# Low parts of the fill tiles' weights, made by a second, adding transfer in place of a subtraction on VectorE

## The chip, the cores and the metric

The kernel runs on one core of one Trainium2 chip. The metric is the device time of one execution in microseconds (us); lower is better. Engines are named as in the profile: PE (TensorE, matrix multiplication), PEld (its weight loads), DVE (VectorE), ACT (ScalarE), POOL (GpSimd), and SP (SyncE), which here only issues transfers (DMAs).

## The reference, cut to what matters

A trunk of two layers over 512 tokens with 1024 channels, in fp32. In each layer the normalized input goes through one wide projection `w_in`; its columns feed four mixers (RWKV7, gated linear attention, a linear recurrence, HGRN2); their outputs are joined, projected by `w_out`, normalized and added; a gated feed-forward block follows.

```python
for l in range(DEPTH):
    h = _rms_norm(x, norm_mix_pre[l])
    proj = h @ w_in[l]
    p_a, p_b, p_c, p_d = _split(proj, (RWKV_COLS, GLA_COLS, LRU_COLS, HGRN_COLS))
...
    mixed = jnp.concatenate([y_a, y_b, y_c, y_d], axis=-1).astype(x.dtype) @ w_out[l]
    x = x + _rms_norm(mixed, norm_mix_post[l])
    h = _rms_norm(x, norm_ffn_pre[l])
    gate, up = jnp.split(h @ ffn_w_gate_up[l], 2, axis=-1)
    x = x + _rms_norm((jax.nn.silu(gate) * up) @ ffn_w_down[l], norm_ffn_post[l])
```

## The kernel before, in words

**Products in three parts.** Every large product is computed as three products of parts. A weight tile of 128 output columns by 1024 inputs is loaded as `ws` (512 KB, L387, a transfer issued by SP). ACT rounds it to the high part `wh` (L388), and DVE subtracts, `wl = ws - wh`, the low part (L389). The activations are split likewise into `hh` and `hl`. For each of the eight 128-row blocks k, `mm3` (L398) issues wh·hh, wl·hh, wh·hl: 24 matmuls for a tile, and already the second one reads `wl`. All this is one helper, `load_w`, used for every weight.

**Fill tiles.** In each layer the work between the input normalization and `w_out` is called the merge here: 62 to 291 us of the span in layer 0 and 756 to 991 us in layer 1. There the generator `fill()` makes the column tiles of `w_in` still missing (20 for each layer go through its call of `gemm`), while four generators make the mixers: `rwkv`, `hgrn`, `gla`, `lru`. `merge` takes steps from these five by a string of digits, one string for each layer (`ORDER`; 0 is the fill, 1 to 4 the mixers). That sets the order in which the program is written. A scheduler, which simulates the engines while the program is built, then sets the order of the instructions on each engine from it. Once set, each engine runs its instructions strictly in that order, so one that waits holds up those behind it. The same holds for the transfers that POOL issues: they stand in POOL's own row of instructions.

**Memory.** Tiles live in 47 blocks, given out and reused; a tile name such as `block_wl` in the profile says what stands in a block at that time.

**Lines named further down.** L608 to L610 compute the RWKV decay (DVE, then ACT with loads of its function tables); L656 the first product of its blocks (`A`), L952 a product on POOL that L955 (`dk`) reads on PE; L734 a masking on POOL that L742 (`ap`) reads; L759 and L808 (DVE) rearrange blocks for L829 (`pq` on PE); L707 (`dot`) is a small product on PE; L1060, L1179 and L442/L443 are ACT functions at the mixers' ends; L1250 takes a finished fill tile out of PE's accumulators.

## Time and profile before

| | us |
|---|---|
| median of three runs | 1411.95 |
| lowest and highest | 1409.92 to 1412.04 |
| the profiled execution's own time | 1410.65 |
| its span in the trace | 1408.9 |
| busy in the span: PE | 1359.2 (96%) |
| busy: DVE | 792.9 (56%) |
| busy: ACT | 633.5 (45%) |
| busy: POOL | 81.0 (6%) |

The span runs from the first to the last recorded instruction. A busy share is an average over stages of different kinds: in the feed-forward stages PE is nearly always busy; in the two merges it has to share the time with long chains of small instructions on DVE, ACT and POOL. "PEclk" in a table by stretches is the granted clock of PE as a share of the full one (1.00 is 2.4 GHz, 0.50 is 1.2 GHz).

### The profile page before, as it was taken

How to read it: one execution, taken by the hardware profiler on the slowest of the kernel's cores; microseconds unless marked ns; L12 is line 12 of the kernel's file. 1: busy time of each engine (PE TensorE's matmuls, PEld its weight loads, DVE VectorE, ACT ScalarE, POOL GpSimd, SP SyncE). 2: the span in 40 equal slices, each digit the busy share in tenths (PEclk: the TensorE clock that was granted, in tenths of full speed). 3: DMA queues.
4: the chain of work that ended last, by engine and by line, in shares of the span. 5: the costliest groups of instructions: out<-in, count | busy, mean ns of one | idle time of the engine just before them, and what ended most of it. 6: DMA issues, size and time to landing. Idle time of an engine off the chain costs nothing.

```text
span 1408.9 us, 20225 instructions
## 1 busy us (share of the span) xinstructions
PE 1359.2 (96%) x8284; PEld 1150.8 (82%) x8284; DVE 792.9 (56%) x1241; ACT 633.5 (45%) x1035; POOL 81.0 (6%) x71
## 2 busy tenths in 40 slices
PE   7999998999999999999999999989999999999996
PEld 7877877779988888888897778776998888888886
DVE  7598848746834344412666996586286444433234
ACT  6546458555623232322556374676464232223232
POOL 0130102000000000000002300120000000000000
PEclk9989999999999999999999899999999999999999
DMA  7101202314422222433542111133053313233342
GB/s 269 59 30 30 75 16 90 92 46 135 165 90 90 75 90 75 145 91 94 173 149 60 45 45 61 40 96 107 24 171 116 124 45 114 70 101 121 106 130 85
DMA packets 51692, 131.75 MB, mean 94 GB/s; under 512 B 4752, under 2 KB 23776, under 8 KB 51600
## 3 DMA queue, kind: packets, MB, share of 16 engines
q1 hardware_dynamic: 50400, 128.47, 28.5%
q8 instruction: 65, 1.06, 0.3%
q10 hardware_dynamic: 960, 0.95, 0.2%
q0 software_dynamic: 240, 1.05, 0.2%
q14 instruction: 27, 0.22, 0.0%
HBM read 122.06 MB, written 8.39 MB: 93 GB/s over the span
## 4 chain that ended last, share of the span: by engine, by line
PE 79%; DVE 9%; ACT 8%; DMA 2%; issue 2%; POOL 0%; SPq 0%; DVEq 0%; ACTq 0%; POOLq 0%
PE g L398 69%; PE lv L999 2%; DMA block_ws<-in_w_in_dram 1%; DVE block_wl L389 1%; PE nrm L451 1%; ACT block_wh L388 1%; DVE block_att L1005 1%; DMA block_x<-in_xT_dram 1%; PE A L656 1%; PE px L836 1%; ACT block_ws L994 0%; PE ap L742 0%; DVE block_ws L1018 0%; PE pq L829 0%; ACT L1179 0%
## 5 line engine op out<-in xcount | busy, mean ns | idle before, releaser
L398 PE MATMUL g<-block_h,block_wh 128*128 128x512 f32 (+1 forms) x1738 | 496.7, 364 | 9.0 <-ACT block_h L479 7.6
L398 PEld LDWEIGHTS g<-block_h,block_wh 128*128 128x128 f32 x1738 | 317.1, 192 | 61.6 <-ACT block_h L479 8.1
L398 PE MATMUL g<-block_h,block_wl 128*128 128x512 f32 (+1 forms) x1126 | 340.8, 360 | 0.7 <-DVE block_wl L389 0.6
L398 PE MATMUL g<-block_wl,block_wh 128*128 128x512 f32 (+1 forms) x827 | 255.7, 353 | 0.2 <-ACT block_wh L388 0.2
L398 PEld LDWEIGHTS g<-block_h,block_wl 128*128 128x128 f32 x1126 | 210.3, 192 | 32.6 <-DVE block_wl L389 1.9
L388 ACT CAST block_wh<-block_ws 128x1024 fp32r<-128x1024 f32 (+1 forms) x124 | 128.4, 1038 | 226.2 <-DMA block_ws<-in_w_dn_dram 66.2
L398 PE MATMUL g<-block_wl,block_wl 128*128 128x512 f32 (+1 forms) x607 | 184.9, 351 | 0.0
L398 PEld LDWEIGHTS g<-block_wl,block_wh 128*128 128x128 f32 x827 | 151.4, 191 | 22.8 <-ACT block_wh L388 1.0
L389 DVE TENSOR_TENSOR block_wl<-block_ws,block_wh 128x1024 fp32r<-128x1024 f32 (+1 forms) x82 | 102.9, 1257 | 83.6 <-ACT block_wh L388 68.2
L398 PEld LDWEIGHTS g<-block_wl,block_wl 128*128 128x128 f32 x607 | 111.1, 190 | 15.4 <-issue 0.7
L388 ACT CAST block_wl<-block_ws 128x1024 fp32r<-128x1024 f32 (+1 forms) x46 | 47.4, 1031 | 93.6 <-PE g L398 35.4
L398 PE MATMUL g<-block_g,block_wl 128*128 128x512 f32 (+1 forms) x314 | 82.5, 344 | 0.0
L398 PE MATMUL g<-block_g,block_wh 128*128 128x512 f32 (+1 forms) x280 | 81.2, 347 | 0.0
L389 DVE TENSOR_TENSOR block_wl<-block_ws,block_wl 128x1024 fp32r<-128x1024 f32 (+1 forms) x32 | 38.1, 1191 | 50.1 <-ACT block_wl L388 45.8
L398 PEld LDWEIGHTS g<-block_g,block_wl 128*128 128x128 f32 x314 | 53.6, 189 | 7.2 <-issue 0.2
L398 PEld LDWEIGHTS g<-block_g,block_wh 128*128 128x128 f32 x280 | 48.6, 189 | 6.6 <-issue 0.2
L389 DVE TENSOR_TENSOR block_wh<-block_ws,block_wh 128x1024 fp32r<-128x1024 f32 (+1 forms) x29 | 34.6, 1192 | 32.8 <-ACT block_wh L388 27.2
L398 PE MATMUL g<-block_wh,block_wh 128*128 128x512 f32 (+1 forms) x145 | 46.6, 342 | 0.0
L398 PE MATMUL g<-block_wh,block_wl 128*128 128x256 f32 (+1 forms) x133 | 37.9, 337 | 0.4 <-DVE block_wl L389 0.4
L580 POOL TENSOR_SCALAR block_sq<-block_sq 64x512 f32<-64x512 f32 x2 | 1.2, 618 | 579.1 <-DVE block_cum L1250 521.2
L398 PE MATMUL g<-block_h,block_y 128*128 128x512 f32 x90 | 33.7, 389 | 0.0
L398 PE MATMUL g<-block_g,block_h 128*128 128x512 f32 (+1 forms) x100 | 33.0, 366 | 0.0
(1096 smaller groups left out, 2122.1 us busy)
## 6 DMA issues: line engine op xcount, KB each, us to landing
block_ws<-in_w_gu_dram SPq DMA_DIRECT2D x78, 512.0 KB, 3.6
block_ws<-in_w_in_dram SPq DMA_DIRECT2D x48, 512.0 KB, 3.7
block_ws<-in_w_dn_dram SPq DMA_DIRECT2D x39, 512.0 KB, 3.6
block_ws<-in_w_dn_dram SPq DMA_DIRECT2D x18, 384.0 KB, 3.1
xs<-block_x SPq DMA_DIRECT2D x18, 256.0 KB, 3.9
block_x<-xs SPq DMA_DIRECT2D x18, 256.0 KB, 4.0
block_x<-in_xT_dram SPq DMA_DIRECT2D x14, 256.0 KB, 5.3
block_ws<-in_w_out_dram SPq DMA_DIRECT2D x6, 512.0 KB, 3.7
```

The lines of the kernel that those rows point to most:

```text
L388: nc.scalar.copy(out=wh, in_=ws)
L389: nc.vector.tensor_sub(out=wl, in0=ws, in1=wh.bitcast(F32))
L398: nc.tensor.matmul(ps, lhsT=w[:, i, :], rhs=h[i], start=(first and n == 0), stop=(last and n == len(steps) - 1))
L451: nc.tensor.matmul(ps, lhsT=self.ones, rhs=acc[:, s], start=(s == 0), stop=(s == 1))
L580: nc.gpsimd.tensor_scalar(out=low[64:128, :], in0=low[64:128, :], scalar1=0.5, scalar2=0.5, op0=ALU.mult, op1=ALU.add)
L656: nc.tensor.matmul(ps[:, j * P:(j + 1) * P], lhsT=bk[ct][p0:p0 + 64, c_ * P:(c_ + 1) * P], rhs=ar[ct][p0:p0 + 64, c_ * P:(c_ + 1) * P], st ...
L836: nc.tensor.matmul(ps[:, g * P:g * P + P], lhsT=n21[h][:, g * P:(g + 1) * P], rhs=pq[h][:, g * P:g * P + P], start=True, stop=True)
L999: nc.tensor.matmul(ps[:, j * nh * 64:(j + 1) * nh * 64], lhsT=Kt[ct][:, g * P:(g + 1) * P], rhs=qr[:, g].rearrange("p h c -> p (h c)"), st ...
L1005: nc.vector.copy_predicated(out=av[:, :, :, 1, :], mask=m, data=pv)
```

## The change

For the fill tiles alone, `load_w` no longer subtracts on DVE. ACT writes the negative of the high part, `wl = -wh`, and then POOL issues a second transfer of the same 512 KB of `w_in` from HBM, which adds what it brings to what stands in `wl`: again ws - wh. All other weights keep the subtraction. The two strings of `ORDER` are altered too.

```diff
-    def load_w(self, src, nk):
+    def load_w(self, src, nk, adding=False):
...
             nc.sync.dma_start(out=ws, in_=src)
             nc.scalar.copy(out=wh, in_=ws)
-            nc.vector.tensor_sub(out=wl, in0=ws, in1=wh.bitcast(F32))
+            if adding:
+                nc.scalar.activation(out=wl, in_=wh.bitcast(F32), func=AF.Copy, scale=-1.0)
+                nc.gpsimd.dma_start(out=wl, in_=src, accum_op=ALU.add)
+            else:
+                nc.vector.tensor_sub(out=wl, in0=ws, in1=wh.bitcast(F32))
...
-    def gemm(self, src, hs, nk=KD, c=slice(0, T), later=0, keep=None):
+    def gemm(self, src, hs, nk=KD, c=slice(0, T), later=0, keep=None, adding=False):
...
-                w = self.load_w(src[:, k0:k0 + n, :], n)
+                w = self.load_w(src[:, k0:k0 + n, :], n, adding)
...
-                    ps = self.gemm(d["w_in"][l, base[grp] + i], hs, later=0 if grp == "rw" else PG)
+                    ps = self.gemm(d["w_in"][l, base[grp] + i], hs, later=0 if grp == "rw" else PG, adding=True)
```

Of the strings, this is the first third of layer 1's, before and after:

```diff
-0111110111011010210121241210401224124404102212212240241421102222202212102211012013211
+0111110111011010210121241210401422412440102212212240241421102222202212102211012013211
```

In the program's order DVE loses 40 instructions (1195 to 1155), ACT gains 40 (938 to 978) and POOL 40 (76 to 116). The lines of the changed kernel lie about five further on (L398 becomes L403, L1250 becomes L1255); L391 is the negation, L392 the adding transfer.

The first place is the last fill tile of layer 0 (`g_99`, at 220 us of the trace). On ACT, before and after; `wh_73` is the tile's high part, `wl_102` its low part, `qk` an activated gate, `sq` the squares for a normalization:

```order
L388 CAST block_wh_73_1477<-block_ws_7_572 128x1024
L1179 ACT_TABLE_LOAD
L1179 ACTIVATE block_qk_5_803<-block_qk_5_803 128x512
L1060 ACTIVATE block_sq_2_284<-o_62_1861 128x512
L418 CAST block_y_19_2005<-block_prw_2_8_281 128x512
```

```order
L389 CAST block_wh_73_1491<-block_ws_7_573 128x1024
L1184 ACT_TABLE_LOAD
L1184 ACTIVATE block_qk_5_809<-block_qk_5_809 128x512
L391 ACTIVATE block_wl_102_1992<-block_wh_73_1491 128x1024
L1065 ACTIVATE block_sq_2_284<-o_62_1879 128x512
L423 CAST block_y_19_2025<-block_prw_2_8_281 128x512
```

The negation stands behind the gate's activation and ahead of the squares. At the same place on PE, before and after:

```order
L702 MATMUL tr_113_1966<-cst,block_bk_31_819 128x128 x4
L398 MATMUL g_99_1972<-block_h_17_122,block_wh_73_1477 128x512
L398 MATMUL g_99_1972<-block_h_17_122,block_wl_102_1973 128x512
L398 MATMUL g_99_1972<-block_h_17_122,block_wh_73_1477 128x512
L398 MATMUL g_99_1972<-block_h_19_125,block_wh_73_1477 128x512
```

```order
L707 MATMUL tr_113_1985<-cst,block_bk_31_825 128x128 x4
L403 MATMUL g_99_1991<-block_h_17_122,block_wh_73_1491 128x512
L712 MATMUL dot_114_2028<-block_tots_9_821,cst 128x512
L403 MATMUL g_99_1991<-block_h_17_122,block_wl_102_1992 128x512
L403 MATMUL g_99_1991<-block_h_17_122,block_wh_73_1491 128x512
```

`dot`, which stood behind the tile, now stands between its first matmul and the one that reads the low part.

The second place is a fill tile in the middle of layer 1 (`g_71`, at 856 us). On POOL after, where before only L722 and L734 stood (here L727 and L739):

```order
L727 TENSOR_TENSOR block_qr_27_6625<-block_ws_7_5997,block_sq_3_5658 128x1024
L727 TENSOR_TENSOR block_qr_27_6625<-block_nt_35_6294,block_n_17_43_6389 128x1024
L739 TENSOR_TENSOR block_nst_60_6653<-block_nst_60_6653,cst 128x512
L392 DMA block_wl_74_6886<-in_w_in_dram 128x1024
L392 DMA block_wl_79_7006<-in_w_in_dram 128x1024
L392 DMA block_wl_84_7076<-in_w_in_dram 128x1024
```

The tile's adding transfer stands behind L739. On PE there, before and after:

```order
L398 MATMUL g_66_6739<-block_wl_346_4726,block_wh_68_6741 128x512
L398 MATMUL g_71_6852<-block_h_2_5384,block_wh_73_6853 128x512
L398 MATMUL g_71_6852<-block_h_2_5384,block_wl_74_6854 128x512
L999 MATMUL lv_34_6723<-block_ws_52_6467,block_ws_17_5725 128x128 x4
L742 LDWEIGHTS block_m_16_6451
L742 MATMUL ap_71_6786<-block_nst_60_6623,block_m_16_6451 128x32
```

```order
L747 LDWEIGHTS block_n_17_43_6389
L747 MATMUL ap_71_6818<-block_nst_60_6653,block_n_17_43_6389 128x32
L688 MATMUL tr_74_6837<-cst,block_x_339_4704 128x128 x4
L403 MATMUL g_71_6884<-block_h_2_5402,block_wh_73_6885 128x512
L403 MATMUL g_71_6884<-block_h_2_5402,block_wl_74_6886 128x512
```

The tile's first use of its low part moved behind `ap` and `tr`.

The third place is the last fill tile of layer 1 (`g_99` again, at 911 us). On DVE, before and after; `qr` is what `pq` reads:

```order
L1250 TENSOR_TENSOR block_sr_41_6361<-g_99_7373,block_rstd_409_5212 128x512
L419 TENSOR_TENSOR block_wl_79_6973<-block_tots_9_6212,block_wl_79_6973 128x512
L795 TENSOR_TENSOR block_m_16_6451<-ap_106_7290,block_nst_60_6623 128x512
L1017 TENSOR_TENSOR block_ws_17_5725<-block_ws_17_5725,block_ig_8_6408 128x128x2
L759 STREAM_TRANSPOSE block_qr_23_6530<-block_m_16_6451 128x512
L1181 TENSOR_TENSOR block_ig_8_6408<-block_ig_8_6408,block_sr_41_6361 128x512
L419 TENSOR_TENSOR block_y_19_7408<-block_ws_17_5725,block_y_19_7408 128x512
L808 COPY block_qr_27_6595<-block_qr_23_6530 32x8x32 x4
```

```order
L800 TENSOR_TENSOR block_sq_3_5658<-ap_106_7326,block_nst_60_6653 128x512
L1255 TENSOR_TENSOR block_n_17_43_6389<-g_94_7343,block_rstd_409_5230 128x512
L764 STREAM_TRANSPOSE block_ws_12_6050<-block_sq_3_5658 128x512
L1070 SCALAR_TENSOR_TENSOR block_tots_9_6236<-o_62_7300,half,block_ws_330_4666 128x512
L813 COPY block_qr_27_6625<-block_ws_12_6050 32x8x32 x4
L1071 TENSOR_TENSOR block_tots_9_6236<-block_tots_9_6236,block_qk_5_6224 128x512
L969 TENSOR_TENSOR block_ws_17_5743<-block_ws_17_5743,block_qk_10_6246 128x512
L424 TENSOR_TENSOR block_wl_79_7006<-block_tots_9_6236,block_wl_79_7006 128x512
L1255 TENSOR_TENSOR block_sr_41_6388<-g_99_7412,block_rstd_409_5230 128x512
```

The copies for `pq` (L808, now L813) stood behind the last tile's way out (`sr`, L1250) and now stand ahead of it (L1255).

## Rows read from the trace of the kernel before

**Rows 1.** Stretches: length, busy us (count) of PE, PEld, DVE, ACT, POOL; PEclk, DMA share, GB/s.

```profile
62.00:291.00 229.00, 215.08 (x1599) 169.43 (x1598) 175.53 (x302) 136.24 (x217) 36.50 (x29) 0.96 0.18 57
756.00:991.00 235.00, 221.79 (x1647) 174.44 (x1646) 176.49 (x306) 139.55 (x223) 41.65 (x30) 0.96 0.19 61
...
92.00:122.00 30.00, 28.83 (x123) 23.65 (x122) 29.97 (x56) 9.83 (x20) 6.41 (x4) 0.78 0.00 1
122.00:152.00 30.00, 30.00 (x158) 23.55 (x157) 24.91 (x45) 20.02 (x28) 2.15 (x1) 1.00 0.18 54
786.00:816.00 30.00, 30.00 (x133) 24.41 (x133) 29.89 (x54) 11.45 (x25) 10.22 (x6) 0.83 0.06 18
```

**Rows 2.** Groups of lines L388 and L389 (count: ns min/median/max, first and last start).

```profile
L388 ACT CAST block_wh<-block_ws x124: 831/1049/1057, 5.4 to 1382.4; 128x1024 fp32r<-128x1024 f32 x118, 128x768 fp32r<-128x768 f32 x6
L389 DVE TENSOR_TENSOR block_wl<-block_ws,block_wh x82: 953/1221/2912, 6.4 to 1379.2; 128x1024 fp32r<-128x1024 f32 x79, 128x768 fp32r<-128x768 f32 x3
```

**Rows 3.** Chain of waits through layer 0's merge (start, length, what).

```profile
69.71 2.32 DVE block_wl L389
...
91.65 2.83 DVE block_wl L389
...
101.72 1.13 DVE block_wl L389
```

**Rows 4.** Timeline of ACT, both layers (in brackets the idle time before, and its releaser).

```profile
74.80 0.63 ACT L609 ACTIVATE block_cum<-block_cum 128x512 f32<-128x512 f32 x1 [1.31 <-DVE block_cum L608]
...
772.60 0.63 ACT L609 ACTIVATE block_ws<-block_ws 128x512 f32<-128x512 f32 x1 [0.91 <-DVE block_ws L608]
```

**Rows 5.** Timeline of PE: the three longest waits in the merges' first thirds.

```profile
87.16 1.18 PE L955 MATMUL dk<-cst,block_qk 128*128 128x2 f32 x8 [1.98 <-POOL block_qk L952]
...
112.38 2.07 PE L656 MATMUL A<-block_x,block_x 64*128 64x128 f32 x8 [1.17 <-DVE block_prw L662]
...
784.87 1.05 PE L955 MATMUL dk<-cst,block_qk 128*128 128x2 f32 x8 [2.47 <-POOL block_qk L952]
```

**Rows 6.** Timeline of POOL: the issue of a transfer.

```profile
2.23 0.54 POOL L316 DMA_DIRECT2D cst<-in_consts_dram  x1
```

**Rows 7.** Transfers (issuer, count, KB each, median us to landing).

```profile
block_ws<-in_w_in_dram SPq DMA_DIRECT2D x48, 512.0 KB, 3.7
...
cst<-in_consts_dram POOLq DMA_DIRECT2D x1, 788.0 KB, 7.8
```

**Rows 8.** Timelines of ACT and PE at the last fill tile, layer 0.

```profile
217.26 0.63 ACT L1179 ACTIVATE block_qk<-block_qk 128x512 f32<-128x512 f32 x1
...
220.17 0.39 PE L398 MATMUL g<-block_h,block_wl 128*128 128x512 f32 x1
...
226.33 1.02 PE L707 MATMUL dot<-block_tots,cst 128*128 128x512 f32 x2
...
229.63 2.02 PE L829 MATMUL pq<-block_bmat,block_qr 128*128 128x128 f32 x16 [1.49 <-DVE block_qr L808]
```

**Rows 9.** Timelines of PE and POOL, middles of both merges.

```profile
156.43 2.33 POOL L722 TENSOR_TENSOR block_qr<-block_nt,block_m 128x1024 f16<-128x1024 f32 x1
...
165.70 0.40 PE L398 MATMUL g<-block_h,block_wl 128*128 128x512 f32 x1
...
851.15 2.09 POOL L734 TENSOR_TENSOR block_nst<-block_nst,cst 128x512 f32<-128x512 f16 x1 [4.91 <-DVE block_nst L732]
...
858.55 0.48 PE L398 MATMUL g<-block_h,block_wh 128*128 128x512 f32 x1
```

**Rows 10.** Timelines of ACT and PE at the last fill tile, layer 1.

```profile
910.73 0.60 ACT L1060 ACTIVATE block_ws<-o 128x512 f32<-128x512 f32 x1
...
910.97 0.39 PE L398 MATMUL g<-block_h,block_wh 128*128 128x512 f32 x1
917.66 0.56 PE L742 MATMUL ap<-block_nst,block_ws 128*128 128x32 f16 x16
...
928.62 1.62 PE L829 MATMUL pq<-block_bmat,block_qr 128*128 128x128 f32 x6 [4.12 <-DVE block_qr L808]
```

More of the change, by code (lines that the diff above doesn't have):

```diff
@@ L84 @@
 PRI = {'fill': 0, 'rw': 0, 'hg': 0, 'gl': 0, 'lr': 50}
-ORDER = ('0111101111011010210121241120401224124404102212242102414212102222202121210221102013211021031140113034333313033113131313113131313103311122113103131111111111', '0111110111011010210121241210401224124404102212212240241421102222202212102211012013211021031141313034331330331113131431313131333011312131111311313111111111')
+ORDER = ('011110111101101021012124112040122412440410221224210241421210222220212121022110201321102103114011303433331303311313131311313131310331112211310313111111111', '0111110111011010210121241210401422412440102212212240241421102222202212102211012013211021031141313303431330331113131431313131330113121331111311313111111111')
 LATE = 100
```

## The prediction

> **What bounds the kernel now.** I read four views: the table by stretches, the groups by line, the chain of waits, and the timelines around the waits it names. Only the two merges are touched. In the table [rows 1] PE is busy 215.08 of 229.00 us in layer 0's merge and 221.79 of 235.00 us in layer 1's: 13.9 and 13.2 us are all the PE time that shorter chains elsewhere could give back by ending waits. DVE is busier in the early stretches than on the mean: 29.97 of 30 us from 92 to 122 us and 29.89 from 786 to 816 us, so there it is DVE that sets the pace of the mixers. In the same two stretches PE, though busy, runs at a granted clock of 0.78 and 0.83 of 2.4 GHz. From 122 to 152 us PE is busy 30.00 of 30 at 1.00: what is saved or spent beside it there is worth nothing.
>
> The groups by line [rows 2] give the prices: a cast of a whole tile on ACT 1.05 us, a subtraction on DVE 1.22 us (median), at most 2.91 us. The chain of waits [rows 3] has three subtractions of layer 0's first part on it, two of them far longer than the median.
>
> **What is removed.** 40 subtractions, 20 in each layer: 40 x 1.22 = 49 us of DVE. How little of it is worth something, the places show.
>
> *Layer 0, first part.* The subtraction at 69.71 (2.32 us) stands ahead of L608, for which ACT's L609 waited 1.31 us [rows 3, 4]. Behind 1.31 us less, L609 meets the end of its own table load, which the tile's new negation on ACT (1.05 us, partly in an idle gap) pushes back by an estimated 0.3 us: gain 1.0 us. Then 2.83 and 1.13 us at 91.65 and 101.72 go: by 112 us DVE is 1.0 + 2.8 + 1.1 = 5.0 us earlier. PE, however, can gain only what it waits: at 87.16 it waited 1.98 us at the end of this chain, at 112.38 1.17 us [rows 5]. The first wait shrinks by 1.0, the second goes: **-2.2 us**. Besides, the granted clock of 0.78 means (1 - 0.78) x 30 = 6.6 us of full-speed work lost from 92 to 122 us [rows 1], in spells that follow these two waits. Bounds: nothing of it back, or all of it. I take a quarter, since only the shorter of the two waits vanishes: **-1.7 us**.
>
> *Layer 1, first part.* The same place waits 0.91 us (L609 for L608) [rows 4]; the wait of PE behind it is 2.47 us and shrinks by 0.9 [rows 5]. Clock: (1 - 0.83) x 30 = 5.1 us lost; the wait ahead of it stays over half its length, so I take a fifth, 1.0. Together **-1.9 us**.
>
> *Middle parts.* Nothing: PE is full [rows 1], and this is also the cover for the negations there.
>
> **What is added.** 40 negations on ACT of 1.05 us (the nearest row is the cast of the same tile [rows 2]): 42 us. ACT is busy 136 of 229 and 140 of 235 us, so most lie in idle time; a few stand in ACT's rows of table loads that the chain of waits runs through. Without the cover of a full PE each of those would cost 1.05 us.
>
> 40 transfers of 512 KB issued by POOL. An issue took POOL 0.54 us [rows 6]: 22 us on an engine that is busy 78 of 464 us in the merges. The DMA queues, busy 18 to 19% there [rows 1], take 21 MB more without becoming a bound. What counts is the time to landing, for the matmul behind waits for it, with all PE work behind that. No row of before shows an adding transfer. Bounds: the plain one of the same size from SP lands in 3.7 us; from POOL 788 KB landed in 7.8 us, at the start among many others [rows 7]. The size says the lower, the issuer the upper; I take 5.0 us, nearer the first because the merges' queues are emptier than the start. With the issue this is D = 5.5 us from a finished negation to a usable low part. By the Trainium skill ("DMA: Bandwidth & Descriptors", Anatomy of one DMA — SWDGE (gpsimd) path) a plain transfer from POOL takes 2.0 us and its bytes at 436 GB/s, so an estimated 3.2 us for 512 KB. By that estimate the sum below would be near -9.9 us, about 1402. No run here shows it for one that adds.
>
> Most negations end 11 us and more before PE reads the tile (by the times of before, in the new order), so D is hidden. Four places are tighter:
>
> *Last tile, layer 0.* The negation stands behind the gate's activation, which ended at 217.89 [rows 8], so it ends at 218.94; the low part is there at 218.94 + 5.5 = 224.5. PE read it at 220.17, and `dot` (1.02 us) is now put in between: 3.3 us late. Behind the tile `pq` waited 1.49 us anyway: **+1.8 us**; in general D - 3.7.
>
> *A tile in the middle of layer 0.* Its transfer stands on POOL behind the product that ended at 156.43 + 2.33 = 158.76; PE read it at 165.70 [rows 9]: hidden until D = 6.9.
>
> *A tile in the middle of layer 1.* Its transfer stands behind L734, which ended at 853.24; the tile's start, now behind `ap` and `tr`, comes at about 858.55, its low part's use 0.2 us later [rows 9]: late by D - 5.5, now **0**.
>
> *Last tile, layer 1.* On ACT cast and negation now stand about L1060, which ended at 911.33 [rows 10]: 911.33 + 2 x 1.05 = 913.4, and with D 919.0. The tile takes PE 6.7 us (910.97 to 917.66), so it ends at 925.5, and `pq` can follow after some 0.9 us. But `pq` started only at 928.62, after a wait of 4.12 us for L808 [rows 10]; these copies now stand ahead of the tile's way out on DVE. So even the late tile lets `pq` start earlier: **-2.2 us**, in general D - 7.8.
>
> **The sum.** -2.2 - 1.7 - 1.9 + 1.8 + 0 - 2.2 = -6.2 us. Against the profiled execution's own 1410.65 us this is 1404.5 us; the median of the runs lies 1.3 us higher, so the forecast is **1405.8 us**. 0.2% is 2.8 us, about what a measurement of this kernel can tell from no change (its three runs lie 2.1 us apart).
>
> **The rivals.**
>
> *Late landings (slower).* Place: the four tight tiles. As D grows, they cost D - 3.7, D - 6.9, D - 5.5 and D - 7.8 on top of -5.8 for the two first parts. At the slowest landing of before, 7.8 us (D = 8.3): 4.6 + 1.4 + 2.8 + 0.5 - 5.8 = +3.5 us, 1415.5 us. It is faster by over 2.8 us while the landing stays under 6.1 us, and slower by over 2.8 us from 7.6 us on. For it: whether adding costs a transfer extra, no row tells, and the negations and transfers are queued behind other work on two engines that run in order. Against it: 3.7 us for the plain one. Chance 0.20.
>
> *POOL and DVE hold each other up.* A subtraction of 1.22 us took 2.91 us when POOL worked on a product beside it [rows 2], so the two engines do slow each other. If an issue on POOL waits as long for DVE, D becomes 5.5 + 2.9 = 8.4 at the tight tiles, with the same 1415.5 us. It would need such a meeting at the tight tiles, where DVE has no instruction of such length in every case: chance 0.05. The Trainium skill ("SBUF — State Buffer", Who interferes with whom) states that a DVE instruction with two inputs in SBUF contends with a POOL instruction that reads SBUF, and that a transfer issued by POOL can starve behind DVE while its descriptors are written. The trace agrees with the first by the 2.91 us; no run here shows the second.
>
> *The gain is waited off later (no change).* The first parts' 5.8 us exist only if ACT, the transfers and the blocks' release also move forward behind 122 us. The next stage starts with a transfer and a row of table loads on ACT, into which a negation is put; if that row ends when it did before, PE only reaches its next wait sooner. Then the tails alone remain: +1.8 - 2.2 = -0.4, 1411.6 us. For it: PE is full from 122 us on, so nothing hurries it. Against it: what PE does in these 30 us is work that must be done in any case, and that is done sooner. Chance 0.23.
>
> *The clock comes back whole (faster still).* If PE no longer falls to half speed in the two stretches, 6.6 + 5.1 = 11.7 us return in place of 2.7: -15.2 us, 1396.8 us. Against it: two waits of over an us remain. Chance 0.10.
>
> **How the numbers follow.** The forecast has 0.42. Faster by over 0.2%: forecast and whole clock, 0.52. Within 0.2%: 0.22 (the gain waited off). Slower: 0.26 (late landings, the two engines). The likeliest case's own range is 1402 (half the clock back) to 1409 us (landing at 6.1 us). For 8 in 10 I go down to 1398, which cuts off most of the whole clock, and up to 1417, 1.5 us beyond the slower rivals.
>
> **What the new profile would show.** Landings of the adding transfers near 5 us; PE's wait before L656 in layer 0 gone and those for `dk` at 1.0 and 1.6 us; DVE some 49 us less, ACT 42 us more; a wait of some 3 us of PE for the last tile of layer 0; a higher granted clock from 92 to 122 us. Wrong would be the prediction if landings take 8 us, if waits of PE for low parts stand at tiles other than the four, or if L609's table loads start no earlier.

## The result, and the profile of the changed kernel

The changed kernel takes 1419.34 us (median of four runs, 1417.74 to 1420.53), the kernel before beside it 1411.39 (1409.92 to 1412.04): ratio 1.0057, 95% interval 1.004 to 1.0074. It is slower by 8 us; 1405.8 was forecast, and the range ended at 1417. Of a kernel below (old strings, last tiles subtracting) one run of twelve took 2694 us and is left out.

The profiled execution took 1417.74 us, its span is 1416.0. First the page of the changed kernel, its lines on the engines and two on transfers (the last number is the median us to landing):

```profile
PE 1358.5 (96%) x8284; PEld 1147.5 (81%) x8284; DVE 747.2 (53%) x1201; ACT 670.0 (47%) x1075; POOL 114.0 (8%) x111
...
block_ws<-in_w_in_dram SPq DMA_DIRECT2D x47, 512.0 KB, 4.4
...
block_wl<-in_w_in_dram POOLq DMA_DIRECT2D x34, 512.0 KB, 5.6
```

Then its stretches, with the columns of [rows 1]:

```profile
62.00:291.00 229.00, 215.11 (x1614) 168.36 (x1613) 160.84 (x292) 152.15 (x234) 50.33 (x42) 0.97 0.36 86
756.00:991.00 235.00, 215.84 (x1620) 169.88 (x1619) 160.76 (x289) 143.37 (x226) 48.55 (x43) 0.96 0.37 91
92.00:122.00 30.00, 30.00 (x132) 23.81 (x131) 25.87 (x56) 15.02 (x27) 10.21 (x6) 0.83 0.34 56
786.00:816.00 30.00, 29.24 (x138) 22.79 (x136) 29.19 (x57) 14.94 (x28) 10.35 (x8) 0.91 0.37 70
```

The work moved as costed: DVE has 45.7 us less (49 forecast), ACT 36.5 more (42), POOL 33 more (22; an issue took 0.86 us, not 0.54). PE is as busy as before, so it *waits* more: in layer 1's merge it was busy 221.79 of 235 us [rows 1] and now is 215.84.

Where it waits, the chain of waits says. These are its pieces that are transfers, from layer 0's last fill tile to the end of layer 1's merge (start, length, what):

```profile
216.99 5.57 DMA block_wl<-in_w_in_dram
...
695.35 5.43 DMA block_ws<-in_w_in_dram
...
753.97 4.96 DMA block_ws<-in_w_in_dram
...
868.09 5.86 DMA block_ws<-in_w_in_dram
...
912.92 5.46 DMA block_wl<-in_w_in_dram
...
977.67 3.48 DMA block_ws<-in_w_out_dram
...
984.72 5.12 DMA block_cum<-in_w_out_dram
```

Two are adding transfers (`block_wl`), those of the last fill tile of either layer. The load at 753.97 stands ahead of layer 1's first chain, the one at 984.72 at layer 1's end; in the kernel before the first took 3.50 us and the second was not on the chain. Measured by the same instructions of PE, the changed kernel is 2.8 us *ahead* of the profiled run of before from 300 to 700 us and 6.6 us *behind* from 1000 us on: in this execution the loss is made in layer 1.

*Layer 1's last fill tile.* PE's timeline of the changed kernel around it (idle time before and its releaser in brackets):

```profile
914.45 0.47 PE L403 MATMUL g<-block_h,block_wh 128*128 128x512 f32 x1
918.43 0.80 PE L403 MATMUL g<-block_h,block_wl 128*128 128x512 f32 x1 [3.50 <-DMA block_wl<-in_w_in_dram]
919.02 0.63 PE L403 MATMUL g<-block_h,block_wh 128*128 128x512 f32 x1
...
926.64 1.02 PE L712 MATMUL dot<-block_tots,cst 128*128 128x512 f32 x2
927.50 0.95 PE L960 MATMUL dk<-cst,block_qk 128*128 128x4 f32 x8
928.31 2.03 PE L834 MATMUL pq<-block_bmat,block_qr 128*128 128x128 f32 x16
930.18 0.95 PE L988 MATMUL pp<-cst,block_qk 128*128 128x4 f32 x8
...
931.96 1.03 PE L1004 MATMUL lv<-block_ws,block_n 128*128 128x256 f32 x4
```

The low part lands 3.50 us late. Behind the wait the matmuls take 0.63 us each, not 0.39, until 924 us, since PE has dropped to its lower level; the stretches show the granted clock (the last three columns as in [rows 1]):

```profile
914.50:918.40 3.90, 0.42 (x3) 0.11 (x1) 2.44 (x6) 3.85 (x8) 2.22 (x4) 0.91 0.83 140
918.40:924.40 6.00, 5.97 (x14) 4.72 (x15) 2.37 (x5) 2.54 (x4) 2.78 (x3) 0.50 0.37 98
```

0.50 is 1.2 GHz. And in order behind the tile stand `dk`, `pp` and `lv` (L1004); the chain of waits runs on from the tile through all three. The first row of `lv` stands 39.4 us behind `gz` (L1115, at 892.53, the product for GLA's gate); in the kernel before it was 30.8 us.

### The profile page after: what moved, and what is told of

The parts are those of the page before. It is cut to its first block, busy times and chain, and to the rows that moved or that the text cites. A ratio compares the mean times of both kernels' runs of the same rounds, so it can differ in the third digit from the quotient of the medians.

```text
span 1416.0 us, 20369 instructions
## 1 busy us (share of the span) xinstructions
PE 1358.5 (96%) x8284; PEld 1147.5 (81%) x8284; DVE 747.2 (53%) x1201; ACT 670.0 (47%) x1075; POOL 114.0 (8%) x111
## 4 chain that ended last, share of the span: by engine, by line
PE 79%; DVE 7%; ACT 6%; DMA 3%; issue 3%; POOL 1%; SPq 0%; DVEq 0%; POOLq 0%; ACTq 0%
PE g L403 70%; PE lv L1004 2%; DMA block_ws<-in_w_in_dram 1%; DVE block_att L1010 1%; PE nrm L456 1%; DMA block_wl<-in_w_in_dram 1%; PE A L661 1%; ACT block_wh L389 1%; DVE block_nst L730 1%; DMA block_x<-in_xT_dram 1%; PE ap L747 0%; PE lg L1160 0%; PE pp L988 0%; ACT L615 0%; DMA block_cum<-in_w_out_dram 0%
## 5 line engine op out<-in xcount | busy, mean ns | idle before, releaser
L403 PE MATMUL g<-block_h,block_wh 128*128 128x512 f32 (+1 forms) x1786 | 496.6, 363 | 9.2 <-ACT block_h L484 7.5
L403 PEld LDWEIGHTS g<-block_h,block_wh 128*128 128x128 f32 x1786 | 323.4, 192 | 64.7 <-ACT block_h L484 8.0
L403 PE MATMUL g<-block_h,block_wl 128*128 128x512 f32 (+1 forms) x968 | 300.6, 362 | 7.2 <-DMA block_wl<-in_w_in_dram 6.2
L389 ACT CAST block_wh<-block_ws 128x1024 fp32r<-128x1024 f32 (+1 forms) x124 | 128.4, 1038 | 207.0 <-DMA block_ws<-in_w_dn_dram 61.4
L403 PE MATMUL g<-block_wl,block_wh 128*128 128x512 f32 (+1 forms) x671 | 213.3, 360 | 0.0
L403 PEld LDWEIGHTS g<-block_h,block_wl 128*128 128x128 f32 x968 | 183.0, 193 | 35.6 <-DMA block_wl<-in_w_in_dram 7.4
L403 PE MATMUL g<-block_wl,block_wl 128*128 128x512 f32 (+1 forms) x461 | 142.6, 350 | 0.4 <-DVE block_wl L394 0.4
L403 PEld LDWEIGHTS g<-block_wl,block_wh 128*128 128x128 f32 x671 | 124.8, 191 | 19.6 <-issue 1.8
L403 PEld LDWEIGHTS g<-block_wl,block_wl 128*128 128x128 f32 x461 | 85.7, 192 | 12.2 <-issue 1.2
L403 PE MATMUL g<-block_g,block_wh 128*128 128x512 f32 (+1 forms) x310 | 89.9, 354 | 0.0
L403 PE MATMUL g<-block_wh,block_wh 128*128 128x512 f32 (+1 forms) x275 | 87.1, 348 | 0.8 <-ACT block_wh L423 0.8
L394 DVE TENSOR_TENSOR block_wl<-block_ws,block_wh 128x1024 fp32r<-128x1024 f32 (+1 forms) x44 | 54.9, 1249 | 62.1 <-ACT block_wh L389 56.1
L403 PE MATMUL g<-block_g,block_wl 128*128 128x512 f32 (+1 forms) x307 | 84.6, 341 | 0.0
L403 PE MATMUL g<-block_wh,block_wl 128*128 128x512 f32 (+1 forms) x210 | 65.2, 346 | 0.4 <-DVE block_wl L394 0.4
L394 DVE TENSOR_TENSOR block_wh<-block_ws,block_wh 128x1024 fp32r<-128x1024 f32 (+1 forms) x33 | 39.4, 1196 | 47.1 <-ACT block_wh L389 31.3
L389 ACT CAST block_wl<-block_ws 128x1024 fp32r<-128x1024 f32 (+1 forms) x35 | 35.8, 1024 | 57.1 <-PE g L403 24.4
L403 PEld LDWEIGHTS g<-block_g,block_wh 128*128 128x128 f32 x310 | 54.0, 190 | 7.8
L403 PEld LDWEIGHTS g<-block_g,block_wl 128*128 128x128 f32 x307 | 52.8, 190 | 6.3
L403 PEld LDWEIGHTS g<-block_wh,block_wh 128*128 128x128 f32 x275 | 50.5, 190 | 7.3 <-ACT block_wh L423 1.0
L392 POOL DMA_DIRECT2D block_wh<-in_w_in_dram x5 | 4.3, 869 | 519.2 <-ACT block_rstd L433 476.8
L389 ACT CAST block_h<-block_ws 128x1024 fp32r<-128x1024 f32 (+1 forms) x19 | 18.4, 971 | 58.5 <-DMA block_ws<-in_w_dn_dram 32.4
L403 PEld LDWEIGHTS g<-block_wh,block_wl 128*128 128x128 f32 x210 | 38.8, 191 | 5.3 <-DVE block_wl L394 0.6
```

Source lines behind the costliest of these rows:

```text
L389: nc.scalar.copy(out=wh, in_=ws)
L392: nc.gpsimd.dma_start(out=wl, in_=src, accum_op=ALU.add)
L394: nc.vector.tensor_sub(out=wl, in0=ws, in1=wh.bitcast(F32))
L403: nc.tensor.matmul(ps, lhsT=w[:, i, :], rhs=h[i], start=(first and n == 0), stop=(last and n == len(steps) - 1))
```

## The experiments

The **theory** after the result: the late landing of the last tiles' transfers, with what stands behind them in PE's order. **Rivals**: the altered strings by themselves; the negations on ACT; a weight cast on ACT that stands badly; a cost of every transfer alike. The negations are tested only together with the relief of DVE (third kernel below). "Old strings" are the `ORDER` of before. Each time is a median of 5 to 12 runs, the ratio is against the kernel before on the same chip (its medians there: 1409.3 to 1410.7), with its 95% interval. Every edit also makes the scheduler write another order: between the first and the third kernel below, which differ in the transfers alone, about a tenth of ACT's rows stand elsewhere. So the difference of two kernels holds the order's share as well.

**Strings or transfers.** Four kernels part the two. The first is the changed kernel with the old strings:

```diff
-ORDER = (<as changed>)
+ORDER = (<as before>)
```

> Adding transfers on all fill tiles as in the change, with the two order strings of the kernel before. Theory A (placement at layer 1's end): the change itself gains 2 to 3 us in each layer's first part; the loss of about 8 us between 950 and 995 us comes from where the last w_out loads, their casts and the last split fall in layer 1, which goes with the new order of work. With the old strings the instructions at layer 1's end stand on ACT much as in the changed kernel, so by A it is 1412 to 1420 us, and its trace has the loss again after 950 us. Theory B (late low parts): the adding transfers' landings of 5.6 us and the waits of PE for them (2.7 and 3.5 us) make the loss, whatever the strings: 1417 to 1421 us, with the loss spread over the merges.

Measured: 1413.39 us, 1.0023 (1.0008 to 1.0037). The second is the kernel before with the new strings, the same edit the other way round.

> The subtraction on DVE everywhere as before, with the two new order strings. Theory A: if the strings alone misplace layer 1's end, it is slower than before by 3 to 8 us, 1414 to 1420 us; if it takes the adding to misplace it, within 2 us of before. Theory B: the strings matter little, 1410 to 1413 us.

Measured: 1415.99 us, 1.0043 (1.0027 to 1.0059). The strings alone, without a single adding transfer, cost 5.3 us; with them about 5 to 6 (1419.3 against 1413.4; by the ratios 4.8). They don't cost it at the same places, though. Without adding transfers the last tile of layer 1 is not late, but `pq` behind it waits for DVE's copies, and `lv` stands 38.4 us behind `gz`, nearly as far as in the changed kernel:

```profile
928.34 2.90 PE L829 MATMUL pq<-block_bmat,block_qr 128*128 128x128 f32 x12 [5.52 <-DVE block_qr L808]
```

So a late `lv` alone doesn't show that a transfer made it late; the runs on the last tiles below do. The third has the old strings and leaves the transfers out, so that the low part lacks the weight itself and only the relief of DVE and the negations remain:

```diff
                 nc.scalar.activation(out=wl, in_=wh.bitcast(F32), func=AF.Copy, scale=-1.0)
-                nc.gpsimd.dma_start(out=wl, in_=src, accum_op=ALU.add)
```

> Old strings, ACT writes the negative of the high part, and the adding transfer is left out (so the low part is not the reference's). Against the run of the adding kernel with old strings (1.0023 of before) this takes away the landings, their traffic and POOL's issues, and keeps what DVE gained and ACT pays. Theory A (the transfer's landings and its traffic cost what DVE's relief gives): 1407 to 1410 us, 3 to 6 us less than with the transfers. Rival (DVE's relief is worth nothing and ACT's 42 us cost): 1412 to 1415 us, as with the transfers.

Measured: 1406.6 us, 0.9974 (0.9965 to 0.9984). So the relief, the negations' cost taken off, is real, 3.6 us, and the transfers, with the order that goes with them, take 6.8 us (1413.39 - 1406.6), all of it and more. The fourth leaves out the negation and the low part's block too (the high part stands in for the low one):

```diff
-            ws, wh, wl = (self.u4(n, t) for n, t in (("ws", F32), ("wh", F32R), ("wl", F32R)))
+            ws, wh, wl = (self.u4(n, t) if not adding or n != "wl" else None for n, t in (("ws", F32), ("wh", F32R), ("wl", F32R)))
...
-                nc.scalar.activation(out=wl, in_=wh.bitcast(F32), func=AF.Copy, scale=-1.0)
-                nc.gpsimd.dma_start(out=wl, in_=src, accum_op=ALU.add)
+                wl = wh
```

> Old strings; fill tiles have no low part at all: the high part stands in its place in the matmuls (so PE does the same work), with no subtraction, no negation, no transfer, and no block for it. This bounds from above what taking the subtractions off DVE can be worth. By the prediction's terms for the first parts of both layers (2.2 + 1.7 + 1.9 us) and the freed blocks: 1403 to 1407 us. Rival (the gain is waited off later): within 2 us of before, 1409 to 1413 us.

Measured: 1415.9 us, 1.0041 (1.0029 to 1.0053): less work, and slower than before, which neither expectation had. In its trace PE is up to 9.8 us ahead of before in layer 0 and loses this again at the ends of the two merges. The order on every engine is another one; that it is the order that costs the time is likely but not shown.

**Which layer.** The changed kernel, adding in one layer alone, the other layer with its old string and the subtraction:

```diff
-        ... adding=True)
+        ... adding=l == 0)      # the other kernel: adding=l == 1
```

> Adding transfers in layer 0 alone, with the new string for layer 0 and the old one for layer 1. Layer 0 has PE 2.8 us earlier than before in the changed kernel's trace, so both theories expect that gain up to 700 us. Theory A: layer 1 is then as before: 1407 to 1410 us in all, unless its end falls otherwise by itself. Theory B: the same gain, since layer 0 has only one wait of 2.7 us for a low part: 1408 to 1411 us.

> Adding transfers in layer 1 alone, with the old string for layer 0 and the new one for layer 1. Both theories: the loss of layer 1 alone, 9.4 us by the shifts between the two traces (from -2.8 us ahead of layer 1 to +6.6 us behind it): 1419 to 1422 us. Theory A puts 8 us of it behind 950 us of the trace, theory B spreads it from 780 us on.

Measured: layer 0 alone 1411.54 us, 1.001 (0.9992 to 1.0029), no difference; layer 1 alone 1418.78 us, 1.0051 (1.0033 to 1.0069), nearly the whole loss. The 2.8 us that one trace showed in layer 0 is no gain in the medians, and both expectations for layer 0 missed. The two traces show why one of them is not enough. In layer 0 the changed kernel and the one that adds there alone have the same instructions in the same order on every engine, yet behind this layer the first is 2.8 us ahead of before and the second 0.7. At the merge's end the first was granted the full clock and the second was not (columns as in [rows 1]):

```profile
280.00:295.00 15.00, 11.73 (x79) 8.11 (x76) 11.39 (x15) 11.60 (x15) 0.00 (x0) 1.00 0.12 36
280.00:295.00 15.00, 11.73 (x34) 6.83 (x33) 10.27 (x13) 10.88 (x14) 0.00 (x0) 0.77 0.12 36
```

**The last tiles.** All fill tiles add but the last one of each layer, with the old strings and then with the new ones:

```diff
-        ... adding=True)
+        ... adding=(grp, i) != ("lr", 3))
```

> Old strings; adding transfers on all fill tiles but the last of each layer, which subtracts on DVE as before. In the adding kernel with old strings PE waited 2.8 us for the low part of layer 0's last tile and 3.9 us for layer 1's. Theory A (these landings at the ends are what the adding costs): 3 to 5 us less than with all, 1408.5 to 1411 us. Rival (behind the last tile other waits end later anyway): within 1.5 us of it, 1412 to 1415 us.

> The changed kernel with its new order strings, in which only the last fill tile of each layer has its low part made by the subtraction again. Theory (the late landing of the last tile's adding transfer holds up the dk and pp matmuls behind it, and with them the chain to the lv matmuls, which sets the end of layer 1): the first lv matmul of layer 1 starts some 3 to 6 us earlier against its gate's first matmul than the 39.5 us of the changed kernel, and the time falls by 4 to 6 us, to 1413 to 1415 us. Rival (with the new strings VectorE's order alone makes lv late, as in the run that had the new strings and no adding, 38.3 us): lv stays at 38 us or more and the time at 1416 to 1419 us.

Measured: old strings 1409.36 us, 0.9997 (0.9983 to 1.001); new ones 1414.3 us, 1.0027 (1.0012 to 1.0042). With the old strings the two last tiles together cost 4.0 us, with the new ones 5.0. PE's timeline of the second kernel at the same place, in the same order as in the changed kernel, shows how:

```profile
915.40 0.48 PE L403 MATMUL g<-block_h,block_wh 128*128 128x512 f32 x1
915.72 0.40 PE L403 MATMUL g<-block_h,block_wl 128*128 128x512 f32 x1
...
920.95 1.02 PE L712 MATMUL dot<-block_tots,cst 128*128 128x512 f32 x2
921.80 0.95 PE L960 MATMUL dk<-cst,block_qk 128*128 128x4 f32 x8
...
926.26 1.03 PE L1004 MATMUL lv<-block_ws,block_n 128*128 128x256 f32 x4
```

From the tile's first matmul to `dk` 6.40 us, in the changed kernel 13.05: 3.5 us of waiting and about 3 us at half clock. `lv` follows 32.8 us behind `gz`.

**A weight cast out of ACT's way.** The changed kernel, with the cast of one `w_out` tile (m = 7), then of three (m from 5), held back behind the mixers' last splits in layer 1:

```diff
-            nc.scalar.copy(out=wh, in_=ws)
+            with (self.tc.issue_after(behind) if behind is not None else nullcontext()):
+                nc.scalar.copy(out=wh, in_=ws)
...
+        ... behind=lasts[0] if l == 1 and m == 7 else None)      # the other kernel: m >= 5
```

> The changed kernel with its new strings; one instruction moves: in layer 1 the ACT cast of the last w_out tile (its block is freed late, its load lands last) goes behind the cast of the mixers' last split, which PE's next products wait for. All other rows of all engines stay in their order. Theory A (the new string for layer 1 leads to this order, and that is most of the loss): 4 to 6 us of the 8 come back, 1413 to 1415 us, and PE's products of w_out start some 4 us earlier, near 982 to 987 us of the trace. Rival (the mixers' end and the late load itself are the loss, the cast's place is nothing): 1417.5 to 1420 us.

> The changed kernel with its new strings; in layer 1 the ACT casts of the last three w_out tiles go behind the casts of the mixers' last splits, ahead of which they had waited for loads that land late (the run with one of them moved was no faster). Only rows of these tiles move, on ACT, DVE and PE. Theory A (casts that wait for late loads hold up the mixers' last normalizations): 3 to 5 us less than the change, 1414 to 1416 us, with PE's shift between 880 and 1000 us down from 6 to 2 us. Rival (what is late is the mixers' own chain in the new order, before any of these casts): 1418 to 1421 us, with the shift at 4 us or more.

Measured: 1421.39 us, 1.0067 (1.0045 to 1.009), and 1427.12 us, 1.0119 (1.0103 to 1.0135). Both misses. In both, casts of late weights still stand in front of the same copy (ACT's copy of `Y`, see below), which begins 5.4 and 5.3 us after `Y` is done, not 6.8. And in their traces 5.8 and 7.1 us of the shift against the changed kernel arise in layer 0, which the edit leaves as it was. So they don't decide what the cast costs; that was told apart by the strings (below).

**Where the gain lies.** With the old strings, adding on four tiles of the first parts alone, and then on all but the last tiles and layer 1's lr0 and lr1 (the linear recurrence's first two tiles), whose transfers run beside the load in front of its first chain:

```diff
+        ... adding=(grp, i) in (("gl", 4), ("hg", 4), ("gl", 5), ("hg", 6)))
+        ... adding=(grp, i) != ("lr", 3) and not (l == 1 and grp == "lr" and i < 2))
```

> Old strings; adding transfers on four fill tiles of each layer alone, those whose subtractions stood on the chain of waits in the first parts (the second to fifth w_in tile loaded after the merge begins); all others subtract. Theory A (the relief of DVE is worth 3.7 us where DVE sets the pace, and the costs come from the last tiles' landings and from loads slowed by the added traffic): 1406.5 to 1409 us, faster than before and than the change. Rival (the first parts' gain is waited off later, and any other order than that of before loses at layer 1's end): 1410 to 1414 us.

> The order strings of before; adding transfers on all fill tiles but the last one of each layer and lr0 and lr1 of layer 1, whose transfers run beside the weight load that layer 1's first chain waits for. Theory (the relief of VectorE is worth some 3.7 us and is eaten by transfers that delay a load in front of a chain or land late behind the last chain; with those left out part of it remains): 1407 to 1409 us, faster than before by 1 to 3 us. Rival (every adding transfer costs about what it saves, wherever it lies): 1410 to 1412 us, as before.

Measured: 1410.52 us, 1.0008 (0.9995 to 1.0021), and 1409.11 us, 0.9992 (0.9982 to 1.0002). Neither is told from the kernel before, and the first theory's range was missed.

**Which part of the strings.** Four kernels whose last tiles subtract, with layer 0's string new; layer 1's new; of layer 1's the early place alone (digits 32 to 40); its late places alone (from digit 98).

```diff
 layer 1, digits 32 to 40
-...210401224124404102...
+...210401422412440102...
```

> Adding transfers on all fill tiles but the last one of each layer, layer 0's order string as changed, layer 1's as before. Theory (what is left of the loss when the last tiles subtract, 1414.3 against 1410.4 us, is layer 1's altered string): 1409 to 1411.5 us. Rival (layer 0's string, one digit shorter at its end, which moves the order at the end of layer 0): 1413 to 1415.5 us.

> As the run before it in this list, but layer 0's string as before and layer 1's as changed. Theory (layer 1's string costs the rest): 1413 to 1415.5 us. Rival (layer 0's): 1409 to 1411.5 us.

> Layer 1's string altered at its early place alone (the digits 32 to 40, where gla's steps are put ahead of the fill and rwkv steps), layer 0's as before; last tiles subtract. Theory (the rest is lost at the end of the merge, where the late places of the string put hgrn's and rwkv's last steps in another order): 1409 to 1411.5 us. Rival (it is lost in the first third, where the early place lies): 1412.5 to 1415.5 us.

> Layer 1's string altered at its two late places alone (from digit 98 on), layer 0's as before; last tiles subtract. Theory (the late places cost the rest): 1412.5 to 1415.5 us. Rival (the early place): 1409 to 1411.5 us.

Measured: 1413.59 us, 1.0025 (1.0011 to 1.0039); 1413.59 us, 1.0023 (1.0009 to 1.0037); 1414.65 us, 1.0024 (1.0011 to 1.0037); 1408.88 us, 0.9998 (0.9984 to 1.0012). Against the old strings (1409.36) each string alone costs about 4 us and both together hardly more (1414.3), so the theory that named layer 1's fell in part; inside layer 1's it is the early place, against what I expected. The trace shows where it acts: not near its own place but at the end of the merge. There ACT's timeline of the changed kernel reads

```profile
985.98 0.62 ACT L423 CAST block_wh<-block_sq 128x512 fp32r<-128x512 f32 x1 [1.55 <-DVE block_sq L1071]
989.93 1.05 ACT L389 CAST block_wh<-block_cum 128x1024 fp32r<-128x1024 f32 x1 [3.34 <-DMA block_cum<-in_w_out_dram]
990.88 1.04 ACT L389 CAST block_wh<-block_ws 128x1024 fp32r<-128x1024 f32 x1
991.83 0.61 ACT L423 CAST block_h<-block_qk 128x512 fp32r<-128x512 f32 x1
992.35 0.57 ACT L918 COPY block_sq<-Y 128x512 f32<-128x512 f32 x1
```

and that of the kernel with the late places alone

```profile
978.41 0.62 ACT L423 CAST block_h<-block_qk 128x512 fp32r<-128x512 f32 x1
978.93 0.58 ACT L918 COPY block_sq<-Y 128x512 f32<-128x512 f32 x1
979.41 1.05 ACT L389 CAST block_wh<-block_cum 128x1024 fp32r<-128x1024 f32 x1
```

L918 copies `Y` out for the last norm of RWKV, the last chain of the merge. In the changed kernel it stands behind a cast whose `w_out` load was issued only at 984.72 (see the chain above), when its block `cum` came free: DVE's L1070 had read that block until 984.69. PE had finished `Y` at 985.6, and the copy began 6.8 us later. In the other kernel `Y` ended at 978.5 and the copy followed after 0.4 us; in the kernel before it was 1.5 us. A wait of ACT for this load stands in front of the copy in every kernel whose string has the early place (the changed one and those of the runs that kept its layer 1 string or this place), but for the one with three casts held back, where the load had landed; it stands in none of the others.

In layer 0 the new string puts a table load of ACT (L1077) and its activation in front of the same copy, which begins 1.96 us after `Y` there and 0.05 us with the old string (1.6 in the kernel without low parts, whose order differs throughout). That holds for a subtracting and for an adding last tile, so it is in the changed kernel too. What it costs there was not parted from the rest: from 300 to 700 us the trace with adding transfers and old strings is 6.4 us ahead of before, that of the changed kernel 2.8.

A table of layer 1's end, from the first row of `gz` to the last `gate` of RWKV (L932, in before L927), worked out from PE's timelines, with the mean granted clock of the stretch:

```
                                                             us              clock
kernel before                                                97.1            0.965
last tile subtracts, without the early place (7 kernels)    93.3 to 94.7    0.982 to 1.000
the same, adding on four tiles of the first part alone       96.0            0.947
last tile subtracts, with the early place (3 kernels)       96.4 to 98.1    0.966 to 0.983
no adding transfer, both strings new                       101.3            0.950
last tile adds, old string                                  98.3            0.983
last tile adds, new string, layer 0 as before              101.6            0.967
changed kernel                                             103.8            0.951
changed kernel, casts held back (2 kernels)                102.4 and 103.5  0.951 and 0.942
```

One of the seven kernels adds in layer 0 alone: its layer 1 has the string and the subtractions of before and yet takes 93.7 us, at a clock of 1.000, so 3 us of such a stretch come and go with the clock and with the order that the scheduler writes. An estimate without the clock's part, the length times (1 - clock) taken off: 93.7 for the kernel before, 91.8 to 93.7 in the second row, 94.7 to 94.8 in the fourth, 96.6 for the adding last tile with the old string and 98.7 for the changed kernel. So both causes show in this estimate as well.

**Both undone.** The changed kernel with two edits in layer 1 alone, the last tile's subtraction and the early place as before; then lr0 and lr1 of layer 1 subtracting too:

```diff
-        ... adding=True)
+        ... adding=(l, grp, i) != (1, "lr", 3))
+        ... adding=not (l == 1 and grp == "lr" and i != 2))      # the second kernel
```

> The changed kernel with two edits in layer 1 alone: its last fill tile subtracts, and the early place of its order string (digits 32 to 40) is as before. Theory (the late landing of layer 1's last adding transfer and the order that the early place brings to the end of layer 1, where ACT's copy of Y stands behind a weight cast that waits for its load, are together the whole loss): 1409 to 1412 us, 7 to 10 us under the changed kernel; from the gate's first product to the last gate of layer 1 93 to 95 us in place of 103.8. Rival (the loss is spread over all adding transfers): 1414 us or more.

> As the run before it in this list, and lr0 and lr1 of layer 1, whose transfers run beside the load ahead of layer 1's first chain, subtract too. Theory (those transfers make PE wait 3.6 to 4.9 us for dk at 785 us in place of 2.5): the wait is 2.3 to 3.0 us and the time 1407 to 1409.5 us, under both kernels. Rival (the wait only moves to the next products of the chain, as it did with the old strings, 3.00 us at 797 us): 1409 to 1412 us.

Measured: 1412.92 us, 1.0021 (1.0009 to 1.0033), and 1409.74 us, 1.0 (0.9986 to 1.0014). For the first kernel the stretch came out as expected (94.3 us), the time a little over: two edits take back 6.4 of the 8 us. The second kernel takes back the rest, but no more; its time lies in the rival's range. The wait for `dk` at layer 1's first chain shows the rival's way; of the first kernel

```profile
785.47 1.87 PE L960 MATMUL dk<-cst,block_qk 128*128 128x2 f32 x8 [4.66 <-POOL block_qk L957]
```

and of the second

```profile
786.12 1.05 PE L960 MATMUL dk<-cst,block_qk 128*128 128x2 f32 x8 [2.32 <-POOL block_qk L957]
...
798.42 1.12 PE L960 MATMUL dk<-cst,block_qk 128*128 128x2 f32 x8 [3.01 <-POOL block_qk L957]
```

The wait shrinks at the first `dk` and turns up at the next, so these rows don't show where the 3.2 us between the two kernels come from; the profiled execution of the second was even the longer one (1412.37 us, that of the first 1410.40). No kernel that computes all parts beat the kernel before.

## Why the prediction was wrong

**The step that failed: "last tile, layer 1: -2.2 us".** Its inputs were right. The low part was forecast usable at 919.0 and was at 918.43, with a D of 5.8 us (negation's end at 912.63) against 5.5; the tile's end was forecast at 925.5 and came at 926.6, the difference being the half clock behind the wait, which I had left out (the tile took 8.2 us behind it, not 6.7). `pq` even started a little earlier, 928.31 against 928.62. What was wrong is the reading of [rows 10]: I took the 4.12 us of `pq`'s wait as the slack of everything behind the tile. In PE's order `dk`, `pp` and `lv` stand behind it too, and they had little: `lv` moved from 923.4 to 931.96, and with the last tiles subtracting it follows `gz` 6.6 us sooner. In place of the -2.2 + 1.8 us of the two last tiles, these cost 5.0 us together (1419.34 against 1414.3), with the old strings 4.0. In the traces all of the 5.0 lies in layer 1: with the last tiles subtracting PE is 1.5 us behind the changed kernel ahead of that layer and 6.4 us ahead of it from 1000 us on.

**The strings, costed at nothing beyond the moves shown.** The early place of layer 1's string costs about 4 us (ratios 1.0023 and 1.0024 against 0.9997 with the old strings), by the end of the merge. I had read the order at three places on which waits of before lay; at this one ACT had hardly waited before.

**Layer 1, first part: -1.9 us.** The wait for `dk`, forecast at 1.6 us, grew from 2.47 [rows 5] to 3.94:

```profile
783.15 1.87 PE L960 MATMUL dk<-cst,block_qk 128*128 128x2 f32 x8 [3.94 <-POOL block_qk L957]
```

PE came to this place 3.2 us earlier than before, the chain only 1.7. What held the chain back is the load at 753.97, ahead of its first activation on ACT: it took 4.96 us with an adding transfer on either side of it, that of before 3.50. The other traces agree: 4.6 to 5.9 us with such transfers (and 3.4 in one), 3.3 to 3.7 without. Then DVE's and POOL's timelines of the changed kernel show, at the chain's head,

```profile
760.12 1.80 POOL L735 MEMSET block_ws<- 128x2048 f16 x1 [0.99 <-ACT block_wh L389]
...
760.62 1.57 DVE L597 TENSOR_SCALAR block_sg<-block_sg 128x512 f32<-128x512 f32 x1 [5.99 <-ACT block_sg L596]
```

L597 took 0.43 us before. POOL's memset fills the block of a loaded tile; it used to start at 769.1, and starts earlier now that ACT's cast is the tile's last reader. It is 1.57 us, too, in the kernel that leaves the adding transfers out. But at its old place the same memset stood beside another instruction of this chain (L1085 took 1.86 us there, as L1090 here 1.02), so its move costs 0.3 us in all. The Trainium skill ("SBUF — State Buffer", Who interferes with whom) states that a `tensor_scalar` can use the port pair that DVE shares with GpSimd, and that the one that comes second then waits for the other's whole instruction: by that rule L597 ends shortly after the memset's end at 761.92, and it ended at 762.19, so the trace agrees. This is the rival "POOL and DVE hold each other up", at a place other than the tight tiles.

**Layer 0, first part: -2.2 - 1.7 us.** Right in direction, as far as one trace tells: the wait before L661 (L656 before) is gone, that for `dk` is 1.50 us (1.0 forecast; the chain of the first products is shorter by 0.5 us, not 1.0), the clock from 92 to 122 us is 0.83 (0.78 before). But the medians give layer 0 no gain, and the relief of both layers, without any transfer, is 3.6 us where I had 5.8. "Only the two merges are touched" was misread, too: 14 of the 40 adding transfers were issued ahead of the two stretches, so that DVE lost only 14.7 and 15.7 us in the merges and the rest outside.

**Last tile, layer 0: +1.8 us.** PE waited 2.72 us for the low part where about 3 was forecast:

```profile
222.60 0.50 PE L403 MATMUL g<-block_h,block_wl 128*128 128x512 f32 x1 [2.72 <-DMA block_wl<-in_w_in_dram]
```

From `gz` to the layer's last gate it is 90.0 us, before 90.7. But three other kernels with the same instructions in the same order in layer 0 took 90.6, 90.7 and 92.7 us, at a lower granted clock, so whether the wait lay beside other slack, as forecast, isn't shown. **Middle parts: 0**, right: PE waited for adding transfers at the two last tiles (2.72 and 3.50 us) and nowhere else. **The landing**: 5.6 us (median; 5.2 to 12.2) against 5.0. With the D of 5.8 us of layer 1's last tile in place of 5.5, the three terms that grow with D move the forecast sum by about 1 us. The rival "late landings" named the place, but priced layer 1's last tile at 0.5 us and asked for landings of 7.6 us to be slower; the loss there came with a low part no later than forecast. Nor were 7.8 us the slowest landing of before: SP's loads of `w_in` took up to 10.4 us in the first 62 us. By the Trainium skill ("DMA: Bandwidth & Descriptors", Anatomy of one DMA — SWDGE (gpsimd) path) it would have been an estimated 3.2 us for a plain transfer; for one that adds the measurement decides.

**What stays open.** The parts don't add up exactly: the intervals of the ratios are some 3 to 6 us wide, and each string costs about 4 us alone but the two hardly more together. Nor is it shown what takes the 3.6 us of relief where neither the last tiles nor the early place cost anything (1409.11 and 1409.74 us). Why the early place makes the load wait for block `cum` was not followed into the scheduler; that it does was shown by the traces with and without it.

## What to carry to other kernels

Slack at one waiting instruction is not slack for all that stand behind the same point: follow each of them in the engine's order to the end of the stage, and take the smallest. A transfer put in place of a short operation moves a product by its landing, some 5.5 us here, so it belongs only where the consumer is farther away than that; on the last tile of a stage it is not, and a load that runs beside it can land later, too. When an order table is altered with an edit, time the table alone: here it cost as much as the edit. And before a gain of a few us is read off one trace, compare the granted clock of the stretch.

## What the runs showed of the hardware

An adding transfer of 512 KB issued by POOL landed after 5.6 us (median of the 40). The median of SP's plain loads of `w_in` rose from 3.7 [rows 7] to 4.4 us, but that is no rise beside the transfers as such: in the merges it is 3.6 us in both kernels, and 4.0 overall where the adding ones are left out. What is longer is the load ahead of layer 1's first chain, with adding transfers on either side: 4.6 to 5.9 us in eleven traces out of twelve, 3.3 to 3.7 without such transfers. An issue held POOL for 0.86 us. PE at rest for 3.5 us ran on at 1.2 GHz for the 6 us behind (0.63 us a matmul, not 0.39). And from run to run of one and the same kernel the time follows the mean granted clock: the changed kernel with subtracting last tiles gave 1408.65 us at 0.987 and 1419.88 at 0.980, so that a single profile tells a few us of a stage only with others beside it. The same instructions in the same order were granted 1.00 and 0.77 of the clock at the end of layer 0's merge.
